# Hybrid trunk layer: start order of the first stage, and three places in the feed-forward part where operand preparation is laid out over other slices

## The chip, the cores and the metric

The kernel runs on one core of one Trainium2 chip. Its engines are TensorE (PE, with its weight loads as PEld), VectorE (DVE), ScalarE (ACT), GpSimd (POOL) and SyncE (SP), which here only issues DMA transfers. Each engine works through its own queue in order and waits on semaphores for the others. The metric is the device time of one execution in microseconds (us). A percentage of it is about 28.7 us.

## The reference

One layer (DEPTH = 1) of an encoder trunk on x of 2048 tokens by 1024 channels, all in float32:

```
mod_all = silu(c) @ ada_w + ada_b                  # six rows of 1024: shift, scale, gate, twice
h = modulate(rms_norm(x, norm_g[0]), sh_m, sc_m)   # h * (1 + scale) + shift
y = stick_breaking_mixer(h, w_qkv, w_o)            # 16 heads of 64, blocks of 128 rows
x = x + gt_m * rms_norm(y, norm_g[1])
h = modulate(rms_norm(x, norm_g[2]), sh_f, sc_f)
g, u = split(h @ w_in);  y = (silu(g) * u) @ w_out # D_FF = 2816
x = x + gt_f * rms_norm(y, norm_g[3])
```

What matters here: before anything can be projected, the modulation (`silu(c) @ ada_w`, columns 0 to 2047 for the first norm) and the row norms of x must exist; the feed-forward part (FFN) multiplies h, 2048 x 1024, by 2 x 2816 columns.

## The kernel before

**Precision and products.** Every matmul operand is split in two fp32r halves: a high part, cast on ACT, and the remainder, subtracted on DVE (sometimes POOL). `mm3` (lines 148 to 150) multiplies high by high, high by low and low by high: three matmuls of 128x128 by 128x512. So each operand tile that PE reads costs one ACT cast and one DVE subtraction beforehand.

**Engine order.** The order on PE, ACT, DVE and POOL is the order in which the program text issues the instructions; SP's order is left to a scheduler. An instruction placed early in the text does not run early unless everything ahead of it in its engine's queue is done. `tick()` is called once per *slice* (one `mm3`); `after(n, f)` puts f into the queues n slices later.

**First stage (lines 702 to 790).** Block 0 of x is four tiles of 128x1024. `x_load` brings them in, `x_square` sums their squares on ACT and has POOL raise the mean to the power -1/2, `x_scale` multiplies by it on DVE; `scale_first` does this for tiles 2 and 3 on ACT instead. The modulation's weights come in quarters q; `ada_chunk` loads a half quarter (1 MB for q = 0), `ada_sum` accumulates weight times silu(c) on DVE (lines 627, 630), `ada_direct` gives PE one chunk to sum itself (line 640), `ada_rest` reduces the DVE sum over partitions on PE (line 647), and `ada_cols_done` adds `b_cols` and multiplies by `gc` (lines 655 to 658). Then come the three projection weights' splits (`weights_high` L668, `weights_low` L673), the transposed and modulated rows (`x_turn` L303, `full_high` L689 and L693, `low` L698), and `first_products`. The loop over q repeats this with the sums of the next quarter. DMA transfers use eight semaphores in turn: the ninth issue waits for the first transfer's landing, and so on.

**Middle.** Attention over units of 128 rows by 512 keys and less, then the output projection of four blocks of 512 rows (`out_projection`). After the last slice of each tile, `after` puts x1's sum (`x1_add`, L878), its squares (`x1_square`), its scaling (`x1_scale`, L892) and eight transpositions with modulation (`h2_turn`, L899 on PE, L903 on ACT, then a store) into later slices. For the last tile of the last block these are held back by `LAST_HELD` slices, so that they run beside the FFN's first groups.

**FFN, first product.** 44 groups n: two halves s of the rows by FC = 22 column blocks f; the second half takes the blocks in reverse, so group 22 uses group 21's left operands again. Each group runs seven products of a Strassen-like scheme, in the order 1, 5, 6, 3, 7, 2, 4, four slices each (28 slices, 84 matmuls). Right operands r (14 pairs m per half, `right_load`, `right_split` L1171 and L1172) serve a whole half; left operands l are made per group from the raw weights `wi` (`left_load` L1182, `left_add` L1196, `left_split` L1213 and L1214). Products 1, 6, 7 and 4 accumulate into one PSUM bank and 5 and 3 into another, so after each product `taken` must read the bank before the next product but one may write it: product 1 is copied on ACT (L1296), 3 is added on DVE (L1348), 7 on DVE (L1352), 2 on DVE (L1355), 4 on DVE (L1364). A silu on ACT follows L1348 (L1349) and L1355 (L1356). POOL multiplies gate by up (`one`, L1360, after L1352) and forms four sums per second group (S, L1314). In ordinary groups ADD_AT and SPLIT_AT say at which slices the next group's left operands are made. ADD_SECOND and SPLIT_SECOND do so for group 1, ADD_LATE and SPLIT_LATE for group 23; the right operands of the second half are loaded and split during groups 21 and 22:

```
if at_next == 3 + 12 * m // 5:
    right_load(1, m)
if at_next == 9 + 12 * m // 5:
    right_split(1, m)
```

**FFN, second product.** Another Strassen-like pass over stored activations; nothing of it is touched.

Of the kernel before, what the change touches and what calls it, by code (L numbers as in the profile page):

```python
# [11 lines left out]
AF = mybir.ActivationFunctionType  # L12
# [7 lines left out]
KC = D // P  # L20
# [6 lines left out]
FC = FF // P  # L27
# [42 lines left out]

H2_STEP = 3

LAST_HELD = 16

HOW = ["aav", "avv", "avv", "avp"]

# [6 lines left out]
def hybrid_trunk_kernel(  # L83
# [15 lines left out]
    nc = tc.nc  # L99
# [67 lines left out]
    def load_weights(p, t, tag="wraw"):  # L167
        raw = att.tile([P, KC, P], F32, name=f"wr{p}_{t}", tag=tag, bufs=BUFS[tag])
        nc.sync.dma_start(raw, wqkv[p, t])
        raws[p, t] = raw  # L170
# [108 lines left out]
    x_tiles, x_norm, x_rstd = {}, {}, {}  # L279

    def x_load(b):
        for i in range(4):
            r0 = b * BT + i * P
            xt = att.tile([P, D], F32, name=f"x{b}_{i}", tag="v", bufs=BUFS["v"])
            nc.sync.dma_start(xt, x[r0 : r0 + P])
            x_tiles[b, i] = xt

    def x_square(b, i):
        xn = att.tile([P, D], F32, name=f"xn{b}_{i}", tag="kt", bufs=BUFS["kt"])
        x_norm[b, i] = xn  # L290
        x_rstd[b, i] = rms_scale(att, x_tiles[b, i], f"n0_{b}_{i}", junk=xn)

    def x_scale(b, i):
        nc.vector.tensor_scalar(
            x_norm[b, i], x_tiles.pop((b, i)), x_rstd.pop((b, i)), None, op0=ALU.mult
        )
# [305 lines left out]
    ON_PE = {0: (0, KC - 1), 1: (KC - 1,), 2: (KC - 1,), 3: (KC - 1,)}  # L602

    def ada_chunk(q, kh):
        ks = range(KC // 2 * kh, KC // 2 * (kh + 1))
        if q == 2:
            for k in ks:
                w = att.tile([P, 2, AQ], F32, name=f"ac{q}_{k}", tag="a", bufs=BUFS["a"])
                nc.sync.dma_start(w, ada_first[q, kh][:, :, k % 4])
                chunks[q, k] = w  # L610
            return
        tag = "ht" if (q, kh) == (1, 1) else "qt"
        w = att.tile([P, 2, KC // 2, AQ], F32, name=f"ac{q}_{kh}", tag=tag, bufs=BUFS[tag])
        nc.sync.dma_start(w, ada_first[q, kh])
        for k in ks:
            chunks[q, k] = w[:, :, k % 4]
# [5 lines left out]
    def ada_sum(q, k):  # L622
        w, scale = chunks[q, k], c_act[:, k : k + 1]
        if q not in piece_sums:
            acc = att.tile([P, 2, AQ], F32, name=f"asum{q}", tag="w", bufs=BUFS["w"])
            piece_sums[q] = acc
            nc.vector.tensor_scalar(acc, w, scale, None, op0=ALU.mult)
        else:
            acc = piece_sums[q]
            nc.vector.scalar_tensor_tensor(acc, w, scale, acc, op0=ALU.mult, op1=ALU.add)  # L630

    def ada_sums(q):
        return [k for k in range(KC) if k not in ON_PE[q]]
# [3 lines left out]
    def ada_direct(q, k):  # L637

        for n, seg, js in COLUMNS:
            nc.tensor.matmul(  # L640
                cols_ps[q][:, n : n + 1], chunks[q, k][:, seg, js], c_act[:, k : k + 1],
                start=False, stop=False, skip_group_check=True,
            )

    def ada_rest(q):
        for n, seg, js in COLUMNS:
            nc.tensor.matmul(
                cols_ps[q][:, n : n + 1], piece_sums[q][:, seg, js], ones[:, 0:1],
                start=False, stop=n == 3, skip_group_check=True,
            )  # L650

    def ada_cols_done(q):

        ps, ms = cols_ps.pop(q), slice(2 * q, 2 * q + 2)
        nc.vector.tensor_tensor(shift[:, 0, ms], ps[:, 0:2], b_cols[:, 0, ms], op=ALU.add)
        sc = att.tile([P, KC], F32, name=f"sc0_{q}", tag="sc", bufs=1)[:, :2]
        nc.vector.tensor_tensor(sc, ps[:, 2:4], b_cols[:, 1, ms], op=ALU.add)
        nc.vector.scalar_tensor_tensor(
            g_eff[:, 0, ms], sc, 1.0, gc[:, 0, ms], op0=ALU.add, op1=ALU.mult
        )  # L660

    def scale_first(i):
        rstd = x_rstd.pop((0, i))
        nc.scalar.activation(x_norm[0, i], x_tiles.pop((0, i)), AF.Identity, scale=rstd)

    def weights_high(t):
        hl = att.tile([P, 2, KC, P], F32R, name=f"w0_{t}", tag="whl", bufs=BUFS["whl"])
        nc.scalar.copy(hl[:, 0], raws[0, t])  # L668
# [34 lines left out]
    nc.scalar.activation(c_act, c_act, AF.Silu)  # L703

    nc.scalar.activation(spare, mhalf, AF.Sigmoid)
    x_load(0)
    ada_chunk(0, 0)
    ada_chunk(0, 1)
    load_weights(0, 1)
    nc.sync.dma_start(b_cols, ada_b_cols)  # L710
    nc.sync.dma_start(gc, g_cols)
# [6 lines left out]
    ada_chunk(3, 0)  # L718
    ada_chunk(3, 1)
    ada_begin(0)  # L720
    x_square(0, 0)
    for i in range(2):
        x_square(0, i + 1)
        x_scale(0, i)
    x_square(0, 3)
    scale_first(2)
    scale_first(3)
    first_acc = {
        1: accps.tile([P, BT], F32, name="pj0_0_1", tag="acc"),
        0: accps.tile([P, BT], F32, name="pj0_0_0", tag="acc"),  # L730
        2: accps.tile([P, BT], F32, name="pj0_0_2", tag="acc"),
    }
    first_h, first_full, stores = norm_h[0], {}, []
    for k in ada_sums(0):
        ada_sum(0, k)
    ada_direct(0, 0)
    turned_x = {m: x_turn(0, m) for m in range(2)}
    ada_direct(0, KC - 1)
    ada_rest(0)
    weights_high(1)  # L740
    weights_low(1)
    ada_cols_done(0)
    weights_high(0)
    weights_low(0)
    full_high(0)
# [7 lines left out]
    for q in range(4):  # L753
        m = 2 * q
# [44 lines left out]
    def after(slices, fn, *args):  # L799

        tasks.append((now + slices, next(serial), fn, args))
# [253 lines left out]
    for s in range(4 * len(units) + last):  # L1055
# [25 lines left out]
        for stage, delay in ORDER_IN_SLOT[s % 2]:  # L1081
            if stage == "proj":
                i = min(s // 4, len(units) - 1)
# [285 lines left out]
    ADD_AT = {0: 5, 5: 6, 8: 3, 11: 7}  # L1369
    SPLIT_AT = {2: 1, 5: 5, 10: 6, 13: 3, 18: 7, 20: 2, 26: 4}  # L1370

    ADD_SECOND = {14: 5, 18: 6, 21: 3, 26: 7}
    SPLIT_SECOND = {15: 1, 17: 5, 21: 6, 25: 3, 32: 7, 35: 2, 40: 4}

    ADD_LATE = {10: 5, 14: 6, 16: 3, 19: 7}
    SPLIT_LATE = {11: 1, 13: 5, 16: 6, 18: 3, 21: 7, 23: 2, 26: 4}

    FIRST_AT = {
        0: [("r", 6)], 2: [("r", 7)], 3: [("l", 7)], 5: [("r", 8)], 7: [("l", 2)], 8: [("r", 9)],
# [7 lines left out]
    for n, (s, f) in enumerate(groups):  # L1387
        banks_of = [bank("x", at, f"s{at}_{n}") for at in (n % 2, 2, 3)]
        if n == FC + 4:
            beside.append(late_modulation((5,), "aT", 2, 1, 8, accps, "acc", "aT", "aT", settle=10, pace=3))  # L1390
        for at, product in enumerate(PRODUCTS):
            acc = banks_of[{1: 0, 6: 0, 7: 0, 4: 0, 5: 1, 3: 1, 2: 2}[product]]
            for k in range(H4):
                hl, r = left[n - (n == FC), product], right[s, product, k]
                mm3(acc, (hl[:, 0, k], hl[:, 1, k]), (r[:, 0], r[:, 1]),
                    k == 0 and product in (1, 5, 2), k == H4 - 1, skip_group_check=True)
                tick()
                t = 4 * at + k
                for what, which in FIRST_AT.get(t, []) if n == 0 else []:
                    first_do[what](0, which)  # L1400
                if t == 3 and n + 2 < len(groups) and n + 2 != FC:
                    left_load(n + 2)
                if n == 0 and t == 0:
                    for fn, at_slice in ((left_add, ADD_SECOND), (left_split, SPLIT_SECOND)):
                        for later, what in at_slice.items():
                            after(max(later, 1), fn, 1, what)
                if 0 < n and n + 1 < len(groups) and n + 1 != FC:
                    add_at, split_at = (ADD_LATE, SPLIT_LATE) if n == FC else (ADD_AT, SPLIT_AT)
                    if t in add_at:
                        left_add(n + 1, add_at[t])  # L1410
                    if t in split_at:
                        left_split(n + 1, split_at[t])
                if s == 0 and 4 <= f < 4 + 2 * H4:
                    kt, second = divmod(f - 4, 2)
                    if t == 5 and not second:
                        sums_load(1, kt)
                    if t in (15, 19):
                        sums_make(1, kt, 2 * second + (t == 19))
                    if t == 25 and second:
                        sums_store(1, kt)  # L1420

                if n in (FC - 1, FC):
                    at_next = t + 4 * len(PRODUCTS) * (n - FC + 1)
                    for m in range(14):
                        if at_next == 3 + 12 * m // 5:
                            right_load(1, m)
                        if at_next == 9 + 12 * m // 5:
                            right_split(1, m)
                if n + 1 == len(groups):
                    if t in B_FIRST:  # L1430
                        b_load(0, B_FIRST[t], "ec")
                    if t - 5 in B_FIRST:
                        b_split(0, B_FIRST[t - 5])
                    if t in (9, 13, 15):
                        a_load((9, 13, 15).index(t))
                    if t in (20, 24):
                        a_split((20, 24).index(t))
            after(1, taken, n, product, banks_of)
# [153 lines left out]
```

## Time and profile before

| what | value |
|---|---|
| time, median of 3 runs | 2873.44 us (2872.65 to 2875.37) |
| the profiled execution | 2873.52 us, of which the span of instructions is 2871.1 us |
| PE busy | 2818.2 us (98%) |
| DVE, ACT, POOL busy | 2027.7, 1634.5, 1280.4 us |
| first stage | 0 to about 46 us of the span |
| FFN groups 0 and 1 | about 1580 to 1621 us |
| FFN groups 21 and 22 | about 1992 to 2036 us |

A line of the timeline reads: start, duration, engine, line, operation, output<-input, shapes, and in brackets how long the engine had been idle before and what released it. A matmul's bar (0.39 us) is longer than the distance between starts (0.23 us), since they overlap; so a stall of PE is read here from the starts. PE's own time at full speed sets nearly all of the span; what can change are the few microseconds in which it waits.

### The profile page before, as it was taken

The numbers are of one execution on the slowest core, as the hardware profiler recorded it, in microseconds if no ns is written. First come the engines' busy times: TensorE is split into PE (matmuls) and PEld (weight loads), VectorE is DVE, ScalarE is ACT, GpSimd is POOL, SyncE is SP. The second block draws the span as 40 slices with busy tenths as digits, with TensorE's granted clock in tenths as the row PEclk, the third lists the DMA queues.
The fourth block names the chain that finished last, engine by engine and source line by source line (L and its number), as shares of the span: only waits on it lengthen the run. The fifth ranks groups of instructions, "written<-read, shape, count | busy, mean of one in ns | idle before, by whom it ended". The sixth has DMA issues, their size and how long they took to land.

```text
span 2871.1 us, 41790 instructions
## 1 busy us (share of the span) xinstructions
PE 2818.2 (98%) x13848; PEld 2335.4 (81%) x13848; DVE 2027.7 (71%) x2821; ACT 1634.5 (57%) x3265; POOL 1280.4 (45%) x2032
## 2 busy tenths in 40 slices
PE   7999999999999999999999999999999999999998
PEld 6788888888888888887888788888778888888887
DVE  6788888888888888888866666555776655134377
ACT  5787777787777877778645533334433333322243
POOL 1465666576576655666410122221222222544454
PEclk9999999999999999999999999999999999999999
DMA  8765546656665635546389544334453335545575
GB/s 324 270 210 165 187 156 223 209 174 227 191 210 184 216 113 175 191 133 227 97 292 313 193 136 151 121 92 163 130 165 118 111 93 175 190 132 153 181 226 186
DMA packets 239367, 516.84 MB, mean 180 GB/s; under 512 B 22320, under 2 KB 110384, under 8 KB 221488
## 3 DMA queue, kind: packets, MB, share of 16 engines
q1 hardware_dynamic: 239152, 514.18, 55.2%
q8 instruction: 109, 1.79, 0.3%
q14 instruction: 106, 0.87, 0.1%
HBM read 346.85 MB, written 118.49 MB: 162 GB/s over the span
## 4 chain that ended last, share of the span: by engine, by line
PE 88%; DVE 5%; DMA 3%; ACT 2%; issue 1%; POOL 0%; SPq 0%; DVEq 0%; POOLq 0%; ACTq 0%
PE s L148 9%; PE s L149 9%; PE s L150 9%; PE o L586 8%; PE z L507 8%; PE t L558 8%; PE pj L148 6%; PE pj L149 6%; PE pj L150 6%; PE o L149 5%; PE o L148 5%; PE o L150 4%; PE y L148 1%; PE y L150 1%; PE y L149 1%
## 5 line engine op out<-in xcount | busy, mean ns | idle before, releaser
L548 POOL TENSOR_TENSOR a<-a,w 128x512 f32<-128x512 f32 (+3 forms) x640 | 620.5, 969 | 221.7 <-DVE w L541 131.7
L541 DVE TENSOR_TENSOR_SCAN w<-z,c,begin 128x512 f32<-128x512 f32 x384 | 489.8, 1279 | 87.1 <-ACT z L526 68.3
L148 PE MATMUL s<-r,l 128*128 128x512 f32 x1232 | 484.5, 393 | 7.0 <-DVE p L1352 4.5
L149 PE MATMUL s<-r,l 128*128 128x512 f32 x1232 | 482.0, 391 | 0.0
L150 PE MATMUL s<-r,l 128*128 128x512 f32 x1232 | 481.8, 391 | 0.0
L524 ACT ACTIVATE a<-z 128x512 f32<-128x512 f32 (+3 forms) x640 | 347.5, 543 | 171.8 <-PE z L507 140.8
L586 PE MATMUL o<-aT,v 128*128 128x512 f32 (+3 forms) x1280 | 387.5, 384 | 0.1
L574 DVE TENSOR_TENSOR aT<-t,aT 128x512 fp32r<-128x512 f32 (+3 forms) x640 | 359.4, 595 | 23.7 <-ACT aT L568 23.2
L507 PE MATMUL z<-kt,qt 128*128 128x512 f32 (+3 forms) x1280 | 363.5, 365 | 0.0
L568 ACT CAST aT<-t 128x512 fp32r<-128x512 f32 (+3 forms) x640 | 314.2, 534 | 75.7 <-PE t L558 65.5
L526 ACT ACTIVATE z<-z 128x512 f32<-128x512 f32 (+3 forms) x640 | 345.1, 539 | 0.0
L1360 POOL TENSOR_TENSOR one<-p,p 128x512 f32<-128x512 f32 x44 | 71.1, 1616 | 595.3 <-issue 307.6
L148 PE MATMUL pj<-ht,w 128*128 128x512 f32 x768 | 312.7, 407 | 7.6 <-ACT ht L693 2.6
L149 PE MATMUL pj<-ht,w 128*128 128x512 f32 x768 | 305.3, 398 | 1.2 <-DVE ht L698 0.7
L558 PEld LDWEIGHTS t<-begin,a 128*128 128x128 f32 x2176 | 255.7, 141 | 58.5 <-DVE aT L574 10.3
L150 PE MATMUL pj<-ht,w 128*128 128x512 f32 x768 | 302.8, 394 | 0.0
L558 PE MATMUL t<-begin,a 128*128 128x128 f32 x2176 | 294.7, 273 | 7.9 <-DVE aT L574 6.8
L148 PEld LDWEIGHTS s<-r,l 128*128 128x128 f32 x1232 | 231.5, 188 | 60.2 <-DVE p L1352 6.3
L150 PEld LDWEIGHTS s<-r,l 128*128 128x128 f32 x1232 | 231.5, 188 | 50.8
L149 PEld LDWEIGHTS s<-r,l 128*128 128x128 f32 x1232 | 231.6, 188 | 50.2 <-issue 0.5
L507 PEld LDWEIGHTS z<-kt,qt 128*128 128x128 f32 x1280 | 230.5, 188 | 40.1
L536 DVE TENSOR_TENSOR_SCAN w<-z,begin 128x128 f32<-128x128 f32 (+3 forms) x256 | 208.7, 818 | 76.4 <-ACT z L526 66.6
(159 smaller groups left out, 4868.1 us busy)
## 6 DMA issues: line engine op xcount, KB each, us to landing
ht<-h_s SPq DMA_DIRECT2D x108, 1024.0 KB, 8.2
wi<-in_win SPq DMA_DIRECT2D x86, 512.0 KB, 4.1
qt<-qn SPq DMA_DIRECT2D x124, 256.0 KB, 4.7
ol_qt<-act_s SPq DMA_DIRECT2D x56, 512.0 KB, 3.7
act_s<-S SPq DMA_DIRECT2D x66, 256.0 KB, 4.2
br<-in_wout SPq DMA_DIRECT2D x66, 256.0 KB, 3.5
h_s<-ht SPq DMA_DIRECT2D x16, 1024.0 KB, 7.8
o_s<-os SPq DMA_DIRECT2D x128, 128.0 KB, 2.4
```

Source lines behind the costliest of these rows:

```text
L148: nc.tensor.matmul(acc, lhs[0], rhs[0], start=first, stop=False, **kw)
L149: nc.tensor.matmul(acc, lhs[0], rhs[1], start=False, stop=False, **kw)
L150: nc.tensor.matmul(acc, lhs[1], rhs[0], start=False, stop=last, **kw)
L507: nc.tensor.matmul(z[:, :n], q[:, e, part, r * P : (r + 1) * P], k[:, e, :n], start=part == 0, stop=part == 1,)
L524: nc.scalar.activation(a[:, :n], z[:, :n], AF.Sigmoid, scale=QK_SCALE)
L526: nc.scalar.activation(z[:, :n], z[:, :n], AF.Sigmoid, scale=-QK_SCALE)
L541: nc.vector.tensor_tensor_scan(rest[:, rev], left[:, rev], begin[:, :BT][:, rev], initial=carries[r], op0=ALU.mult, op1=ALU.bypass,)
L548: nc.gpsimd.tensor_tensor(a[:, :n], a[:, :n], rest[:, 1 : n + 1], op=ALU.mult)
L558: nc.tensor.transpose(pt[:, rb * P : (rb + 1) * P], weighed[i, rb][:, j * P : (j + 1) * P], ident)
L568: nc.scalar.copy(hl[:, 0, t0:], pt[:, t0:])
L574: nc.vector.tensor_tensor(hl[:, 1, t0:], pt[:, t0:], f32(hl[:, 0, t0:]), op=ALU.subtract)
L586: nc.tensor.matmul(acc[:, t0:], lhs, hl[:, part, t0:], start=sc == qb and j == 0 and part == 0, stop=sc == 0 and j == 3 and part == 1,)
```

## The change

1. First stage: the two weight chunks of quarter 0 are loaded ahead of x's four tiles. On the engines the sums of quarter 0, PE's part of them and the reduction come first; x's squares and scalings follow, with `ada_cols_done(0)` in the middle of them; all four tiles are scaled on DVE (`scale_first` is gone).
2. `LAST_HELD` goes from 16 to 30: the last output tile's norm and the eight transpositions of the last block move 14 slices later in the FFN.
3. The left operands of group 23 get the slices that group 1 has (out to slice 40, so into group 23 itself), and in both places the first two splits are a slice later.
4. The right operands of the second half are loaded at slices 4 + 3m and split at 9 + 3m, from group 21's slice 9 to group 22's slice 20 (before: to group 22's slice 12).

```diff
-LAST_HELD = 16
+LAST_HELD = 30
...
-    def scale_first(i):
-        rstd = x_rstd.pop((0, i))
-        nc.scalar.activation(x_norm[0, i], x_tiles.pop((0, i)), AF.Identity, scale=rstd)
...
-    x_load(0)
     ada_chunk(0, 0)
     ada_chunk(0, 1)
+    x_load(0)
     load_weights(0, 1)
...
     ada_begin(0)
-    x_square(0, 0)
+    for k in ada_sums(0):
+        ada_sum(0, k)
+    for k in ON_PE[0]:
+        ada_direct(0, k)
+    ada_rest(0)
     for i in range(2):
-        x_square(0, i + 1)
-        x_scale(0, i)
-    x_square(0, 3)
-    scale_first(2)
-    scale_first(3)
+        x_square(0, i)
+    x_scale(0, 0)
+    ada_cols_done(0)
+    for i in range(2, 4):
+        x_square(0, i)
+        x_scale(0, i - 1)
+    x_scale(0, 3)
...
-    for k in ada_sums(0):
-        ada_sum(0, k)
-    ada_direct(0, 0)
     turned_x = {m: x_turn(0, m) for m in range(2)}
-    ada_direct(0, KC - 1)
-    ada_rest(0)
     weights_high(1)
     weights_low(1)
-    ada_cols_done(0)
...
-    ADD_SECOND = {14: 5, 18: 6, 21: 3, 26: 7}
-    SPLIT_SECOND = {15: 1, 17: 5, 21: 6, 25: 3, 32: 7, 35: 2, 40: 4}
-
-    ADD_LATE = {10: 5, 14: 6, 16: 3, 19: 7}
-    SPLIT_LATE = {11: 1, 13: 5, 16: 6, 18: 3, 21: 7, 23: 2, 26: 4}
+    ADD_LATE = {14: 5, 18: 6, 21: 3, 26: 7}
+    SPLIT_LATE = {16: 1, 18: 5, 21: 6, 25: 3, 32: 7, 35: 2, 40: 4}
...
-                if n == 0 and t == 0:
-                    for fn, at_slice in ((left_add, ADD_SECOND), (left_split, SPLIT_SECOND)):
+                if n in (0, FC) and t == 0:
+                    for fn, at_slice in ((left_add, ADD_LATE), (left_split, SPLIT_LATE)):
                         for later, what in at_slice.items():
-                            after(max(later, 1), fn, 1, what)
...
+                            after(later, fn, n + 1, what)
...
-                        if at_next == 3 + 12 * m // 5:
+                        if at_next == 4 + 3 * m:
                             right_load(1, m)
-                        if at_next == 9 + 12 * m // 5:
+                        if at_next == 9 + 3 * m:
                             right_split(1, m)
```

More of the change, by code (lines that the diff above doesn't have):

```diff
@@ L1402, in hybrid_trunk_kernel @@
                     left_load(n + 2)
-                if n == 0 and t == 0:
-                    for fn, at_slice in ((left_add, ADD_SECOND), (left_split, SPLIT_SECOND)):
+                if n in (0, FC) and t == 0:
+                    for fn, at_slice in ((left_add, ADD_LATE), (left_split, SPLIT_LATE)):
                         for later, what in at_slice.items():
-                            after(max(later, 1), fn, 1, what)
[L1407 to L1412, printed above, removed]
+                            after(later, fn, n + 1, what)
+                if n not in (0, FC) and n + 1 < len(groups) and n + 1 != FC:
+                    if t in ADD_AT:
+                        left_add(n + 1, ADD_AT[t])
+                    if t in SPLIT_AT:
+                        left_split(n + 1, SPLIT_AT[t])
                 if s == 0 and 4 <= f < 4 + 2 * H4:
```

## The prediction

> **What bounds the kernel now.** I read the page first.
>
> ```profile
> span 2871.1 us, 41790 instructions
> ...
> PE 2818.2 (98%) x13848; PEld 2335.4 (81%) x13848; DVE 2027.7 (71%) x2821; ACT 1634.5 (57%) x3265; POOL 1280.4 (45%) x2032
> ...
> PE   7999999999999999999999999999999999999998
> ```
>
> PE is busy in 39 of 40 slices; only waits of PE can be won. Next, PE's waits over the whole run (total, times, longest):
>
> ```profile
> PE acol L640 <- DMA ac<-in_ada_first: 11.7, 1, 11.7
> ...
> PE s L148 <- DVE p L1352: 4.5, 3, 2.6
> PE h2T L899 <- DVE x1n L892: 3.6, 3, 2.0
> ...
> PE s L148 <- ACT p L1296: 2.4, 2, 2.0
> ```
>
> Then the timeline of PE where these lie: groups 0, 0 and 1, then 21 and 22.
>
> ```profile
> 1585.85 0.50 PE L148 MATMUL s<-r,l 128*128 128x512 f32 x1 [0.44 <-ACT p L1296]
> 1598.56 0.51 PE L148 MATMUL s<-r,l 128*128 128x512 f32 x1 [1.45 <-DVE p L1352]
> 1608.71 0.33 PE L899 MATMUL h2T<-begin,x1n 128*128 128x128 f32 x1 [1.98 <-DVE x1n L892]
> 2008.58 0.50 PE L148 MATMUL s<-r,l 128*128 128x512 f32 x1
> 2019.12 0.50 PE L148 MATMUL s<-r,l 128*128 128x512 f32 x1 [2.01 <-ACT p L1296]
> 2032.99 0.50 PE L148 MATMUL s<-r,l 128*128 128x512 f32 x1 [2.61 <-DVE p L1352]
> ```
>
> Against the usual 0.23 us between starts (0.09 for a transposition) PE loses 0.60, 1.62, 2.20, 0.25, 2.16 and 2.78 us: 9.6 us, all that parts 2 to 4 can win. Why, DVE's and POOL's timelines show:
>
> ```profile
> 2007.84 0.69 DVE L1352 TENSOR_TENSOR p<-s,p 128x512 f32<-128x512 f32 x1
> 2008.44 5.78 DVE L1172 TENSOR_TENSOR r<-r 128x512 fp32r<-128x512 f32 x4
> 2014.14 0.68 DVE L1355 TENSOR_TENSOR p<-s,p 128x512 f32<-128x512 f32 x1
> ...
> 2008.94 1.33 POOL L1360 TENSOR_TENSOR one<-p,p 128x512 f32<-128x512 f32 x1 [20.00 <-DMA r<-h_t]
> 2010.36 1.62 POOL L1314 TENSOR_TENSOR S<-one,one 128x512 f32<-128x512 f32 x1
> ```
>
> DVE is full with subtractions of right operands, so the read of a bank (L1355, then ACT's silu, then ACT's copy L1296) comes 5 us late. Four subtractions took 5.78 us beside POOL's products, where four usually take 2.5.
>
> For the first stage, the timeline and the transfers (us to landing last):
>
> ```profile
> 18.58 0.16 DVE L655 TENSOR_TENSOR shift<-acol,b_cols 128x2 f32<-128x2 f32 x1 [0.85 <-PE acol L647]
> 19.09 0.78 ACT L689 ACTIVATE hf<-xT,shift,g_eff 128x512 f32<-128x512 f32 x1 [1.24 <-DVE g_eff L658]
> 23.45 0.48 DVE L627 TENSOR_SCALAR asum<-ac,c_act 128x512 f32<-128x512 f32 x1
> ...
> b_cols<-in_ada_b_cols SPq DMA_DIRECT2D x1, 16.0 KB, 10.9
> gc<-in_g_cols SPq DMA_DIRECT2D x1, 8.0 KB, 10.5
> ```
>
> b_cols (issued 4.74) lands at 15.64 and gc (5.26) at 15.76, behind the first weight (cast at 15.42). From 23.45 DVE's sums run on and PE waits for them at 28.71.
>
> **Part 1, first stage.** SP's order changes by two 1 MB issues passing four 0.5 MB ones; the bytes ahead of the first weight stay, so it still lands at 15.4. x's squares started 1.27 us apart (5.27, 6.54, 7.82, 9.09), which is 0.5 MB of transfer, so now the chunks land at about 6.5 and 9.0 and x's tiles at 10.3, 11.55, 12.8 and 14.1. The later issues wait for landings in turn (gc 6.5, second weight 9.0, third 10.3), and the queue never runs dry.
> DVE: sums (0.48 + 5 x 0.77) done at 11.4; PE's reductions (1.84) at 13.3, hidden. ACT squares (1.06 + 0.19) follow the landings, the last done at 15.4. DVE scales tile 0 at 12.95, then stands at L655 for b_cols until 15.7 and at L658 for gc; behind it, from 16.1, queue two means (0.15 each), three scalings (0.75 each) and POOL's powers (0.55, or 1.02 beside a DVE scaling, as at 7.96): the last scaling ends at 19.2 (before, ACT's pair ended at 12.5). PE's fourth transposition is then out at 19.7, `full_high` ends at 20.5, its cast at 21.1: PE's first product moves from 20.57 to about 21.2. DVE: weight 1 to 20.45, weight 0 to 21.7 (1.23 each), low(0) to 22.4, weight 2 (cast on ACT from 21.1) to 23.6, low(1) to 24.2: the sums start at 24.2, not 23.45. They are what PE waits for at 28.71, so the stage costs **+0.75 us**. Two scalings taken off ACT (2.19 us) are worth nothing: ACT waited 2.95 for the weight behind them. Bounds: if b_cols and gc landed early, scaling would end at 16.9 and the stage would gain 1.2; if POOL's slower power came each time, +1.2.
>
> **Part 2 and part 3 at groups 0 and 1.** The stall of 0.60 is ACT's queue of casts; nothing before it moves. At 1598.56 the wait is L1352. DVE had L1348 at 1594.72, then waited 1.21 for ACT's cast of the second left operand; behind it stood an add and L1352. By slice 18 instead of 17 the add now goes into that wait: L1352 one operation (0.60) earlier, stall 1.0, **-0.6**. The transpositions' wait (2.20): with 30, x1's add, squares and scaling leave the crowded queue. Counting DVE on from L1352 at 1597.2 (0.60 per operation, one at 1.79 beside `one`): adds and splits of groups 1 and 2 to 1607.3, x1's add to 1608.6, its means about 1610, L1348 of group 1 to 1612.5, scaling to 1613.3. PE gets to the first transposition (group 1's slice 20) at 1615.2: 1.9 us to spare, **-2.2**. Of the moved step, ACT's two squares now stand ahead of group 1's copy of product 6 (done 1610.4, needed 1611.7); eight L903 (0.78) stand between copies of groups 1 and 2, each with over a microsecond left. SP's h2 stores (landing 2.0 to 5.6, median 3.3) now share the queue with `one`'s and S's. What is late next: POOL's `one` of group 1 must wait for a buffer until the fourth transposition (group 2's slice 1), some 4 us, and with it its gate buffer, needed at slice 12. Bounds: 1.8 to 3.2 for both.
>
> **Parts 3 and 4 at groups 21 and 22.** Times after group 21's first matmul (1991.93); a slice is 0.69. In DVE's queue L1352 and L1355 of group 21 now stand ahead of two and four right subtractions that they followed. L1352 ends at 15.8 and product 4 needs it at 16.5: the 0.25 goes. L1355 ends at 18.7 (was 22.9), silu at 19.3, casts of r5, r6, r7 to 22.5, copy of product 1 at 23.0; PE needs it at 24.8: the 2.16 goes. Then DVE: r5, r6 and L1364 to 25.1 (POOL costs 1.1 at each subtraction it meets; four meet it), r7 with another meeting to 27.5, r8 to r11 (eight), one add and one split to 33.5, L1348 to 34.1. ACT's silu stands ahead of its casts of r12, so DVE waits 1.3 us there (1.21 in such places before); r12, an add, a split to 37.8, L1352 to 38.4. PE wants product 4 at 35.8: a stall of 2.6 where there was 2.78. So 5.19 becomes 2.6: **-2.6**. After it, the late left operands of group 23 are ready 4 or more us ahead of their products, and copy 1 of group 23 (46.1, needed 46.8) is the tightest. SP: r12's and r13's transfers wait for L1364 (25.1), land by 30, are cast from 34.8. The late raw weights of group 25 load at about 50, land 4.1 later, needed at 60.
> The 1.71 us for a subtraction beside a POOL product is a row of before; that it holds for the moved ones is my choice. Without it DVE would be 4 us earlier and the stall 0 (-5.2); if nothing came of the reordering, 0. I take 2.6 because the same two engines meet at the same products.
> [...]
>
> **Sum:** 0.75 - 0.6 - 2.2 - 2.6 = -4.65 from the profiled execution's 2873.52 (2871.1 of span and 2.4 outside): 2868.9; it lies 0.08 above the median, so **2868.8 us**, 0.16% less. 0.2% (5.7 us) is about what a measurement can tell.
>
> **Rivals.**
> A, DVE catches up: the moved subtractions miss POOL's products, no stall in 21 and 22. For it: two waits of 1.3 us in DVE's queue could absorb POOL's turns. Against: five POOL products fall between 16 and 27, where DVE works. 2873.44 + 0.75 - 2.8 - 5.2 = 2866.2.
> B, the lateness only moves: each operand of group 22 comes just in time for nothing, the total stall stays 5.2. For it: DVE has the same number of operations in these groups. Against: six operations leave the way to L1352 (two right subtractions, two adds, two splits). 2873.44 + 0.75 - 2.8 = 2871.4.
> C, slower: the held h2 pieces. Pieces 5 and 6 on ACT reuse buffers of pieces 3 and 4, whose stores stand on SP behind POOL's `one` and sums. Pieces 3 and 5 are 4.8 us apart; above that, less 1.5 us of slack, ACT holds PE. With the longest landing (5.6), issue and L903 (1.2) and two POOL turns of 1.7 a piece is 5.4 late: 3.9 each for two copies, and as much again for two adds on DVE that wait for the last stores: 15.6 - 4.65 = +11: 2884. Against it: at the median landing of 3.3 no piece is late.
>
> **How the numbers follow.** Forecast 45 in 100, A 25, B 18, C 12. Faster by over 0.2% (under 2867.7) is most of A and a third of the forecast: 0.37; slower (over 2879.2) two thirds of C: 0.08; the rest 0.55. Range: A's 2866.2 less the first stage's lower bound in half, 2865.2; up to B with the stage at +1.2 and the transpositions at their worst, 2873.2; that leaves out C and a little of A.
>
> **What would show it.** First product at about 21.2 and the first quarter-1 sum at 24.2; a DVE wait of about 2 us at L655 for a transfer (if at 18 or later: worse). No wait of PE at L899 in group 1; the wait near 1598 at 1.0 by starts. No wait at product 6 of group 22, one of about 2.6 at product 4 for L1352, four or five right subtractions above 1.7 us. Wrong, if PE waits in groups 2 or 23, which no step of mine foresees, or if the stall at product 4 is under 1 or over 4.

## The result: 0.34% slower, and the profile after

The changed kernel takes 2882.98 us (median of 7, 2880.83 to 2887.51) beside 2873.44 us (median of 7, 2871.66 to 2876.32): ratio 1.0034, 95% interval 1.0022 to 1.0046. The forecast was 2868.8 with a range up to 2873.2. The profiled execution took 2883.78 us. Its page begins:

```profile
span 2881.7 us, 41790 instructions
...
PE 2836.6 (98%) x13848; PEld 2337.5 (81%) x13848; DVE 2029.2 (70%) x2823; ACT 1630.5 (57%) x3263; POOL 1280.0 (44%) x2032
...
PE   8999999999999999999999999999999999999998
```

PE's busy time grew by 18.4 us (2818.2 before) for the same 13848 matmuls. Its waits over the whole run (total, times, longest), the lines that answer to those of before:

```profile
PE acol L640 <- DMA ac<-in_ada_first: 7.0, 2, 6.4
PE s L148 <- DVE p L1348: 3.0, 3, 1.9
...
PE h2T L895 <- DVE x1n L888: 1.1, 2, 0.7
```

The waits on the FFN's banks fell, 4.5 + 2.4 us to 3.0, and the one of 2.0 us for the transpositions is gone. (Lines from about 668 on are 4 lower than before, from about 1400 on 7 lower.) Of the six stalls of before, PE's timeline still shows these two above 0.2 us (the 0.60, which the prediction left in place, is 0.18 here):

```profile
1598.18 0.50 PE L148 MATMUL s<-r,l 128*128 128x512 f32 x1 [0.70 <-DVE p L1348]
...
2031.21 0.47 PE L148 MATMUL s<-r,l 128*128 128x512 f32 x1 [1.93 <-DVE p L1348]
```

So the kernel waits less and takes longer. Setting the start of each of PE's matmuls beside the same matmul of before shows where (a matmul keeps its number, as all of them run in the same order but for a few near the moved parts):

| stretch (by matmul number) | after minus before, us |
|---|---|
| start to 56 us (first stage) | +1.88 |
| attention, 56 to 1500 us | -1.24 |
| to the FFN's start | +0.08 |
| groups 0 to 2 | -3.05 |
| groups 3 to 20 | +3.48 |
| groups 21 and 22 | -2.97 |
| groups 23 to 43 | +3.83 |
| second product | +7.62 |

Together 9.64 us, but for rounding; the 0.9 that the span has beyond that lies behind the last matmul. (Groups 0 to 2 stand in one row, since the transpositions moved from group 1 into group 2.)

The two places that the prediction named for parts 2 to 4 gained what it said and a little more. The loss lies in stretches where nothing was changed and PE doesn't wait. PE's timeline, the first matmul of group 3 and the first of group 20, before:

```profile
1645.85 0.40 PE L148 MATMUL s<-r,l 128*128 128x512 f32 x1
...
1972.70 0.40 PE L148 MATMUL s<-r,l 128*128 128x512 f32 x1
```

and after:

```profile
1643.52 0.39 PE L148 MATMUL s<-r,l 128*128 128x512 f32 x1
...
1973.66 0.39 PE L148 MATMUL s<-r,l 128*128 128x512 f32 x1
```

326.85 us became 330.14 for the same 1428 matmuls: 0.2289 us from start to start became 0.2312. Over the 1848 matmuls of the second product it is 0.2276 and 0.2318. A sum over waits can't show this; only the distance between starts does.

### The profile page after: what moved, and what is told of

It reads as the page before. It is cut to its first block, busy times and chain, and to the rows that moved or that the text cites. A ratio compares the mean times of both kernels' runs of the same rounds, so it can differ in the third digit from the quotient of the medians.

```text
span 2881.7 us, 41790 instructions
## 1 busy us (share of the span) xinstructions
PE 2836.6 (98%) x13848; PEld 2337.5 (81%) x13848; DVE 2029.2 (70%) x2823; ACT 1630.5 (57%) x3263; POOL 1280.0 (44%) x2032
## 4 chain that ended last, share of the span: by engine, by line
PE 91%; DVE 4%; DMA 2%; ACT 2%; issue 1%; POOL 0%; SPq 0%; DVEq 0%; POOLq 0%; ACTq 0%
PE s L148 9%; PE s L149 9%; PE s L150 9%; PE o L586 8%; PE z L507 8%; PE t L558 8%; PE pj L148 6%; PE pj L150 6%; PE pj L149 6%; PE o L149 5%; PE o L150 5%; PE o L148 5%; PE y L148 2%; PE y L150 2%; PE y L149 2%
```

## What differs in those stretches: where the operands lie

Nothing in the code of these groups changed, and the granted clock was 1.0 there in both. What the diff changes for them is the place of the buffers. The pool gives a tag (a named set of rotating buffers) its place when the tag is first asked for, one after the other. In part 1 `ada_begin(0)`, which asks for `w` (three buffers of 2080 bytes, 6240 in all), moved ahead of `x_square`, which asks for `kt` (x's scaled rows; later keys, and operands of both FFN products). `ada_cols_done(0)`, which asks for `sc` (32 bytes), moved ahead of `whl` (weights; later FFN operands). Within a partition, `kt` went from byte 135232 to 141472 and `whl` from 170720 to 170752. Also `v` and `qt` changed places, by whole 4096-byte blocks.

Within the trace of before the pace already went by addresses. In the FFN's first product, 2513 matmuls whose two operands start at the same byte modulo 256 (their neighbours too) are 0.2268 us apart on average, 1068 whose operands start at unlike ones 0.2340 (waits left out). This reading gave the theories that the runs test:

- P: TensorE's pace is set by where its operands start, and part 1 moved them.
- Q: parts 2 to 4 put more work beside the matmuls and slow them.
- R: it is a difference between chips or executions.

## Experiments on the cause of the loss

The kernel before ran beside each group of kernels on the same chip: 2873.23 us (21 runs) beside the first four, 2874.35 (9) beside the four with equal residues or with `kt` 256 bytes off, 2874.43 (31) beside the other four. The ratios are to these.

**Part 1 alone.** The first stage of the changed kernel in the kernel before; `LAST_HELD`, the tables and the loads as before:

```diff
-    x_load(0)
     ada_chunk(0, 0)
     ada_chunk(0, 1)
+    x_load(0)
...
     ada_begin(0)
-    x_square(0, 0)
+    for k in ada_sums(0):
+        ada_sum(0, k)
...
+    x_scale(0, 0)
+    ada_cols_done(0)
...
```

> Part 1 alone (the first stage's new order), parts 2 to 4 as before. Theory P (placement): part 1 changes the order in which buffers are first asked for, and with it the address of the buffers of kt (from 64 to 32, modulo 128 bytes) and of whl (from 96 to 0); TensorE's pace in a stage follows the addresses of its operands. Then this kernel has the whole loss of pace of the changed kernel (about 12.7 us: 1.4 won in attention, 14.1 lost in the FFN and the output product) and the first stage's 1.9, and none of the 4.9 us won at the stalls: 2873.4 + 14.6 = about 2888 us, with matmuls of the last 400 us 0.231 to 0.232 us apart. Theory Q (parts 2 to 4 slow TensorE, by more work beside it): 2875.3 us, matmuls 0.227 us apart at the end.

2886.41 us, ratio 1.0048 (1.0035 to 1.0061). The same two matmuls in PE's timeline:

```profile
1647.31 0.39 PE L148 MATMUL s<-r,l 128*128 128x512 f32 x1
...
1977.45 0.40 PE L148 MATMUL s<-r,l 128*128 128x512 f32 x1
```

330.14 us, to the hundredth what the whole change has: the loss of pace comes with part 1 and needs none of the others.

**Parts 2 to 4 alone.**

```diff
-LAST_HELD = 16
+LAST_HELD = 30
...
+    ADD_LATE = {14: 5, 18: 6, 21: 3, 26: 7}
+    SPLIT_LATE = {16: 1, 18: 5, 21: 6, 25: 3, 32: 7, 35: 2, 40: 4}
...
+if at_next == 4 + 3 * m:
...
```

> Parts 2 to 4 alone (30 for the held step, adds, splits and right operands spread), the first stage as before, so every buffer base as before. Theory P: the 4.9 us won at the stalls of groups 0, 1, 21 and 22 and nothing lost: 2868.5 us, matmuls at the end 0.227 us apart. Theory Q: the pace is lost here too: 2873.4 - 4.9 + 14 = about 2882 us.

2867.89 us, ratio 0.9982 (0.9973 to 0.9991): 5.34 us faster. The same two matmuls, and the stall that is left in group 22:

```profile
1641.95 0.39 PE L148 MATMUL s<-r,l 128*128 128x512 f32 x1
...
1968.80 0.40 PE L148 MATMUL s<-r,l 128*128 128x512 f32 x1
...
2026.06 0.47 PE L148 MATMUL s<-r,l 128*128 128x512 f32 x1 [2.23 <-DVE p L1352]
```

326.85 us, as before. Q falls.

**The addresses alone, both ways.** Unused buffers that shift what comes behind them, and no other edit. In the kernel before:

```diff
+    def pad(name, n):
+        att.tile([P, n], F32, name=f"pad_{name}", tag=f"pad_{name}", bufs=1)
...
+    pad("kt", 24)
     x_square(0, 0)
...
+    pad("whl", 16)
     weights_high(1)
...
+    pad("tmp", 24)
     full_high(0)
```

> The kernel before with unused buffers of 96, 64 and 96 bytes, which bring kt, whl and tmp to the residues that they have after the change (32, 0, 0); no instruction changes. Theory P: 2873.4 + 12.7 = about 2886 us, the FFN and the output product slower by 14 us and attention faster by 1.4. Theory Q, or a difference between chips or executions: 2873.4 us.

2883.69 us, ratio 1.0039 (1.0026 to 1.0052). The same two matmuls:

```profile
1646.16 0.39 PE L148 MATMUL s<-r,l 128*128 128x512 f32 x1
...
1974.94 0.39 PE L148 MATMUL s<-r,l 128*128 128x512 f32 x1
```

328.78 us, where the kernel before has 326.85. With no instruction changed, 256 unused bytes cost 10.5 us: P stands, and R falls. In the changed kernel, the same with 8, 16 and 8:

> The changed kernel with three unused buffers of 32, 64 and 32 bytes, which bring kt, whl and tmp back to the residues modulo 128 bytes that they have before (64, 96, 0), at other absolute addresses; no instruction changes. Theory P, with the residue as what counts: 2883.0 - 12.7 = 2870.3 us. If the absolute address or the order of the buffers counts, or theory Q: 2883 us.

2878.61 us, ratio 1.0018 (1.0009 to 1.0027): 4.4 us won back, not 12.7. A miss: the residue modulo 128 is not the rule. Here `kt` lay at 192 modulo 256 and what it meets at 64, and such pairs were 0.233 us apart on average.

**Equal residues everywhere.** Before, `kt` and most others are at 64, but `whl` is at 224 and `aT` at 0 (modulo 256). One more unused buffer brings them all to 64:

```diff
+    att.tile([P, KC], F32, name="sc_first", tag="sc", bufs=1)
+    pad("whl", 80)
     weights_high(1)
```

> The kernel before with one unused buffer of 320 bytes (and the column sc asked for ahead of it), so that every buffer that a 512-wide matmul reads starts at 64 modulo 512 bytes. No instruction changes. Theory P512 (a matmul takes 0.2267 us where its two operands start at the same residue modulo 512 bytes, and 0.230 to 0.234 where they don't): in the trace of before, matmuls with unlike residues are 2159 of pj, 1134 of s, 1206 of o, 365 of y and 851 of z, at 2 to 7 ns too much; all of them won, 33 us; those that stand beside a transposition not won, 18 us: 2840 to 2855 us. If equal residues are not what counts, 2873 us give or take the 13 us seen between layouts so far.

2857.06 us, ratio 0.9941 (0.9929 to 0.9954): 17.3 us faster than before. The same two matmuls:

```profile
1634.09 0.39 PE L148 MATMUL s<-r,l 128*128 128x512 f32 x1
...
1957.77 0.39 PE L148 MATMUL s<-r,l 128*128 128x512 f32 x1
```

323.68 us, 0.2267 from start to start, the pace of the like pairs of before. The gain falls 2 us short of the range expected: matmuls beside a transposition, in the projections and in the scores stayed at 0.229 to 0.231 on average, although all their operands start at 64 as well. So equal residues alone don't give 0.2267 everywhere.

**The period.** `kt` alone, 256 bytes off the others (`pad("kt", 64)`, and `pad("whl", 16)` in place of 80), then 128 bytes off (32 and 48):

> As the kernel before in the 512-byte layout, but the seven buffers of kt start at 320 modulo 512 (256 bytes off all others). If the period is 512 bytes, matmuls that read a kt buffer (the scores, half of the output product, a quarter of the FFN, half of the projection y) keep 0.230 us or more: about 1280 z, 1008 o, 924 s, 336 y and their neighbours, 4 to 6 ns each, 14 to 21 us slower than with all at 64. If the period is 256 bytes or less, the same time as with all at 64.

> As the kernel before with every operand at 64 modulo 512 bytes (2857.1 us), but the seven buffers of kt start 128 bytes off the others. With 256 bytes off it took the same time, so the period is 256 bytes or a divisor of it. If it is 256: z, half of o, a quarter of s and half of y at 0.230 us or more, about 14 to 21 us slower: 2871 to 2878 us. If it is 128 or less: 2857 us.

256 bytes off: 2857.86 us, and 323.68 us for groups 3 to 20, as with none off. 128 bytes off: 2871.68 us, 14.6 us worse. So what counts repeats every 256 bytes, and operands lie well when they start at the same byte modulo 256. One rival is left: in all these runs the 512-wide matmuls with equal residues have both operands at 64. Whether being equal counts, or this one place, was not tried.

**The change and its parts in that layout.** Parts 2 to 4 with the 320 bytes, and the whole change with the small tags asked for early:

```diff
+    for tag, cols, bufs in (("rms_ssq", 1, 10), ("rms_ms", 1, 4), ("rms_rstd", 1, 4), ("sc", KC, 1)):
+        att.tile([P, cols], F32, name=f"{tag}_first", tag=tag, bufs=bufs)
+    pad("kt", 80)
     for i in range(2):
         x_square(0, i)
```

> Parts 2 to 4 alone, with the same 320 bytes: theory P512 expects the 5.3 us of parts 2 to 4 and the 18 to 33 us of the layout: 2835 to 2850 us; it would beat both kernels. Since TensorE's slices get shorter in front of DVE and ScalarE, up to 2 us of new waits at groups 0, 21 and 22 would be no surprise.

> The changed kernel whole, with buffers asked for in such an order and 320 unused bytes, so that it too has every operand at 64 modulo 512 bytes. Theory P512: within 2 us of the run with parts 2 to 4 alone in the same layout; what differs is the first stage (0.3 us later without a second drop of TensorE's clock, up to 1.9 with it). If something else in the changed kernel slows TensorE, 10 us more than that run.

2850.69 us, ratio 0.9919 (0.9906 to 0.9933), and 2852.56 us, ratio 0.9923 (0.9909 to 0.9936). The changed kernel, freed of its layout, is 30 us faster than as it was written; the version without part 1 is the fastest, 0.8% below the kernel before.

| kernel | kt, whl, aT modulo 256 (others 64) | time, us | groups 3 to 20, us | second product, us |
|---|---|---|---|---|
| before | 64, 224, 0 | 2873.44 | 326.85 | 420.46 |
| after | 160, 0, 0 | 2882.98 | 330.14 | 428.08 |
| part 1 alone | 160, 0, 0 | 2886.41 | 330.14 | 428.08 |
| parts 2 to 4 alone | 64, 224, 0 | 2867.89 | 326.85 | 419.90 |
| before, after's residues modulo 128 | 160, 128, 0 | 2883.69 | 328.78 | 428.09 |
| after, before's residues modulo 128 | 192, 96, 128 | 2878.61 | 329.12 | 426.72 |
| before, all equal | 64, 64, 64 | 2857.06 | 323.68 | 420.16 |
| the same, kt 256 bytes off | 64, 64, 64 | 2857.86 | 323.68 | 419.61 |
| the same, kt 128 bytes off | 192, 64, 64 | 2871.68 | 326.51 | 426.60 |
| parts 2 to 4, all equal | 64, 64, 64 | 2850.69 | 323.68 | 419.52 |
| after, all equal | 64, 64, 64 | 2852.56 | 323.68 | 420.39 |

(The column of groups 3 to 20 runs from the first matmul of group 3 to the first of group 20.) Kernels with the same residues agree there to a hundredth of a microsecond, whatever else differs between them. Why unlike residues cost time was not tried: it stays open.

## Experiments on the steps of parts 2 to 4

Three kernels took one edit each into the kernel before; the residues stay, and groups 3 to 20 took 326.85 us in all three. Stalls are given as the distance of starts less 0.23 (0.09 for a transposition).

**The held step alone** (`LAST_HELD = 30`):

> The kernel before with 30 for the held step alone (it was 16). The prediction's step: TensorE's wait of 2.20 us for the transpositions of x1 goes, the other five stay (0.60 and 1.62 in group 0, 0.25, 2.16, 2.78 in groups 21 and 22): -2.2 us, 2871.2. Its rival C: a wait of 3.9 us or more at a copy of group 1 or 2 comes in its place: 2875 or more. With the wait of 2.2 us, a drop of TensorE's clock for 3.4 us (1.7 us) goes in those executions that have it.

2869.77 us, ratio 0.9987 (0.9977 to 0.9996). PE has no wait at the transpositions of x1. What the prediction left in place is there:

```profile
1597.42 0.51 PE L148 MATMUL s<-r,l 128*128 128x512 f32 x1 [1.06 <-DVE p L1352]
...
2016.07 0.50 PE L148 MATMUL s<-r,l 128*128 128x512 f32 x1 [2.01 <-ACT p L1296]
...
2029.93 0.50 PE L148 MATMUL s<-r,l 128*128 128x512 f32 x1 [2.60 <-DVE p L1352]
```

No copy of groups 1 and 2 waits: rival C falls. By its ratio the kernel gained 3.7 us, more than the 2.2 of the wait. In three of the eight profiled executions that have this wait (part 1 alone, the unused buffers in the kernel before, and the right operands alone) the granted clock was 0.5 for 3.4 us behind it (in that of part 1 alone from 1609.6 to 1613.0 us); that this makes the rest of the gain is argued, not shown.

**Group 23's adds and splits alone:**

```diff
-    ADD_LATE = {10: 5, 14: 6, 16: 3, 19: 7}
-    SPLIT_LATE = {11: 1, 13: 5, 16: 6, 18: 3, 21: 7, 23: 2, 26: 4}
+    ADD_LATE = {14: 5, 18: 6, 21: 3, 26: 7}
+    SPLIT_LATE = {16: 1, 18: 5, 21: 6, 25: 3, 32: 7, 35: 2, 40: 4}
```

> The kernel before with the adds and splits of group 23's operands spread over group 22 as in the change, all else as before. By the prediction's count two adds and two splits (four operations, 0.6 each) leave the way to L1352 of group 22, and none that to L1352 and L1355 of group 21: 0.25 and 2.16 us stay, 2.78 falls to about 0.4: -2.4 us, 2871.0. If DVE's lateness only moves (rival B): the three stay.

2870.46 us, ratio 0.9988 (0.9978 to 0.9997). In PE's timeline the wait at the copy stays, the last one is cut from 2.78 to 1.10 (0.4 expected); the one of 0.25 shows no more:

```profile
2017.29 0.50 PE L148 MATMUL s<-r,l 128*128 128x512 f32 x1 [2.01 <-ACT p L1296]
...
2029.49 0.50 PE L148 MATMUL s<-r,l 128*128 128x512 f32 x1 [0.93 <-DVE p L1352]
```

**The right operands alone:**

```diff
-if at_next == 3 + 12 * m // 5:
+if at_next == 4 + 3 * m:
...
-if at_next == 9 + 12 * m // 5:
+if at_next == 9 + 3 * m:
```

> The kernel before with the right operands' loads and splits spread (every three slices), all else as before. By the prediction's count L1352 and L1355 of group 21 come two and four subtractions earlier, so the waits of 0.25 and 2.16 us go; TensorE then comes 2.4 us earlier to product 4 of group 22, for which only two subtractions (1.2 us) have left the way: its wait grows from 2.78 to about 4.0. Sum -1.2 us, 2872.2. If the meetings with GpSimd fade too (rival A), no more than 2.8 there: -2.4 or better.

2877.09 us, ratio 1.0009 (1.0000 to 1.0019). The waits of 0.25 and 2.16 us are gone and the last grew to 4.20 (4.0 expected), but the time rose instead of falling. Behind this stall PE runs at half speed; first the timeline, then busy time in three stretches (PE, PEld, DVE, ACT, POOL, then granted clock, DMA share, GB/s):

```profile
2034.49 0.77 PE L148 MATMUL s<-r,l 128*128 128x512 f32 x1 [4.04 <-ACT l L1213]
2035.05 0.63 PE L149 MATMUL s<-r,l 128*128 128x512 f32 x1
2035.48 0.63 PE L150 MATMUL s<-r,l 128*128 128x512 f32 x1
...
```

```profile
2028.00:2033.70 5.70, 2.45 (x11) 1.65 (x9) 5.09 (x10) 3.74 (x7) 0.00 (x0) 1.00 0.02 6
2033.70:2040.50 6.80, 6.01 (x14) 4.79 (x15) 5.60 (x9) 2.79 (x5) 1.60 (x1) 0.50 0.33 115
```

For 6.8 us the granted clock is 0.5 and starts are 0.43 apart, not 0.23: about 2.9 us on top of the stall. The right operands pass the lateness on to product 4 of group 22, where the tables of group 23 take part of it away: the stalls of groups 21 and 22 are 3.3 us with the tables alone, 4.2 with the right operands alone and 2.4 with both. By their ratios the held step and the tables alone gained 3.7 and 3.4 us, together more than the 5.2 of parts 2 to 4, and the right operands alone cost 2.6. Whether the kernel is faster without part 4 was not tried.

## Why the prediction was wrong, by its steps

**Parts 2 to 4: right.** Forecast -0.6, -2.2 and -2.6, together -5.4; they measure -5.34 alone. L1352 in group 0: 1.62 to 0.97 with parts 2 to 4 alone and 0.87 in the changed kernel (1.0 forecast); from DVE's L1348 to this L1352 it was 3.10 us before and 2.50 with parts 2 to 4 alone, the one operation that was counted. With the held step alone the stall was 1.22, so not all of the gain need come from that. The transpositions: 2.20 to nothing, as forecast. Groups 21 and 22: 0.25 and 2.16 to nothing, as forecast, and 2.78 to 2.40 with parts 2 to 4 alone (2.09 in the slower-paced changed kernel; 2.6 forecast). The price that carried the 2.6, a subtraction that meets a POOL product, held. In the run with parts 2 to 4 alone DVE's groups of 2, 4 and 8 subtractions between L1352, L1355 and L1364 took 2.39, 4.17 and 5.99 us, where 1.29, 2.50 and 4.9 are usual: 3.9 us of surcharge, 4.4 counted. Rival A (no stall here) and rival B (5.2 us in all) were each off by 2 to 3 us. The two small stalls say nothing for or against it, as they vary without an edit that touches them: the one of 0.25 was gone with part 1 alone and 0.53 with the held step alone, and the one of 0.60, which it held fixed, was 0.19 and 0.74 in these two.

**Part 1: its own working a little high, and one term missing.** DVE's and PE's timeline of the changed kernel:

```profile
15.51 0.16 DVE L655 TENSOR_TENSOR shift<-acol,b_cols 128x2 f32<-128x2 f32 x1 [2.11 <-DMA b_cols<-in_ada_b_cols]
...
23.60 0.48 DVE L627 TENSOR_SCALAR asum<-ac,c_act 128x512 f32<-128x512 f32 x1
...
28.86 1.37 PE L647 MATMUL acol<-ones,asum 128*128 128x1 f32 x8 [0.64 <-DVE asum L630]
```

The wait of 2 us at L655 is as forecast (15.7); the sums start at 23.60, not 24.2, as the last scaling ended at 18.67, not 19.2; PE's wait ends 0.15 us later than before, not 0.75. Then the clock dropped. Stretches of the changed kernel, then of the kernel before:

```profile
26.00:29.40 3.40, 2.76 (x22) 2.35 (x20) 3.26 (x7) 0.00 (x0) 0.00 (x0) 1.00 1.10 384
29.40:36.20 6.80, 6.80 (x19) 5.36 (x19) 6.28 (x14) 2.70 (x4) 0.00 (x0) 0.50 1.01 413
```

```profile
29.00:36.00 7.00, 6.25 (x37) 4.91 (x38) 6.72 (x15) 2.70 (x4) 0.00 (x0) 1.00 1.02 415
```

19 matmuls in 6.8 us where before had 37 in 7.0. This makes most of the 1.88 us of the table. It need not be part 1's doing: with the same first stage, two other kernels of this study had no such drop and were 0.34 and 0.08 us behind at 56 us, and the kernel before too has starts 0.43 us apart in a part of this stage (22.32 to 24.45 us). Whether part 1 makes the drop likelier or longer is not shown. At equal layout the whole change is 1.9 us behind parts 2 to 4 (2852.56 and 2850.69), about what the medians can tell.

**The step that failed** is in the first part: "only waits of PE can be won", with the time of 13848 matmuls taken as given. Part 1's working counted what its moved instructions issue and each queue that they pass, but not that they ask for buffers in another order. That term is -1.24 in attention and +3.48, +3.83 and +7.62 in the FFN, about +13.7 us: more than all six stalls together. (The section on the time before rests on the same step, where it lets only PE's waits change.) It could have been found blind: both programs' buffer addresses are fixed when they are built, and the trace of before holds matmuls of both kinds. Nor was it among the rivals, so the range did not hold it. (The upper bound doesn't come out of its own terms either: rival B with the stage at +1.2 and the transpositions at 1.8 is 2872.8, not 2873.2. Nothing turns on that.) Its check of wrongness (waits in groups 2 or 23) would have missed it as well: no new wait of PE appears.

## What to carry to other kernels

When an edit moves the first use of a buffer, compare addresses as well as instruction orders: here shifts of some hundred bytes moved the time by 0.4 to 0.6%, up or down, with no wait to show for it. When PE is busy all the time, read the distance between the starts of equal matmuls stage by stage; if it varies between stages that do the same, try to let the operands that meet start at the same byte modulo 256 (here all at 64; 320 unused bytes gave 17 us). And cost a stall of PE at more than its length once it nears some microseconds: behind one of 4.2 us the granted clock was 0.5 for 6.8 us here, about 2.9 us on top.

## What the hardware did that was not expected

A matmul's pace followed its operands' start addresses. In the FFN's first product it was 0.2267 us from start to start where all residues modulo 256 bytes are equal, and 0.229 to 0.235 on average with unlike ones (0.2340 in the kernel before, 0.2336 in the changed one), with most single values between 0.224 and 0.240, and the same sum over 1428 matmuls to a hundredth of a microsecond wherever the residues were the same. Equal pairs pay too when unlike ones stand before them: in groups 3 to 19 of the changed kernel they were 0.2283 apart, and in the fifth product of a group, which follows an unlike one directly, two of each three matmuls took 0.231 and 0.232 on average. What happens inside was not looked into.

The granted clock fell to 0.5 behind some stalls and not behind others of the same length: behind the transpositions' stall of 2.1 us with part 1 alone (from 1609.6, for 3.4 us), and not behind the 2.2 us in the kernel before; behind group 22's stall of 2.7 us with parts 2 to 4 in the equal layout (mean granted clock of that execution 0.997), and not behind the 2.4 us in the old one (1.000); for 6.8 us behind the 4.2 us shown above. What decides it was not looked into. It may be a part of what spreads the times of one kernel over several microseconds (the kernel before: 2870.53 to 2878.94 us, with a mean granted clock of 0.996 to 0.999); that is the author's estimate, which no run shows.
